# All four column tiles of xr in one pass over the blocks of x, with the norm's sums and row factors inside the last two blocks

## The chip, the cores and the metric

One kernel on one core of a Trainium2 chip. The metric is the device time of one execution in microseconds (us). A kernel is timed in several runs, and its median counts. Beside the times there is one profiled execution, whose trace gives every instruction with start and duration. TensorE is called PE below, its weight loads PEld, VectorE DVE, ScalarE ACT, GpSimd POOL, and SyncE, which here only issues DMAs, SP.

## The reference

One layer of an encoder, for 512 positions and 1024 channels, in float32. What matters here is its beginning:

```
h = rms_norm(x, attn_norm_g)
proj = h @ w_in
xr, gate, q, k, v = jnp.split(proj, [D_RNN, 2 * D_RNN, ...], axis=-1)
xr = centred_depthwise_conv(xr, conv_w, conv_b)
h_f = rg_lru(xr, ..., False)
h_b = rg_lru(xr, ..., True)
y_rnn = (h_f + h_b) * gelu(gate)
```

`x` is 512 x 1024, `w_in` 1024 x 2560; `xr`, `gate`, `q`, `k`, `v` have 512 columns each. Dilated attention over q, k, v, an output projection, an MLP of width 4096 and a final norm follow.

## The kernel before

A float32 product is done as three passes: each operand is split into a part `hi`, rounded to the matmul's format, and the rest `lo`, and the sum `hi*hi + hi*lo + lo*hi` is accumulated (`mm3`, L303 to L305: three matmuls in a row into one PSUM tile). ACT or DVE makes `hi`, DVE makes `lo`.

**The first stage, xr.** x arrives transposed, in eight blocks of 128 channels x 512 positions (`k` = 0 to 7), and each block is followed in the same transfer by 384 columns of `w_in` for it, that is column tiles 0 to 2 of xr (`xw0` for block 0, in two transfers; `xw` for the others, 448 KB each). SP issues these one after the other. `cvx(k)` splits the block: h_hi = x times the norm's gain (ACT; in blocks 0 and 1 ACT and DVE share it), w3h (the weights' hi part), h_lo and w3l on DVE. `sq(k)` squares the block on ACT, `addsq` adds the squares up on DVE. PE goes through the blocks and for each does three mm3, one per column tile `t` (`pxr[0..2]`); in blocks 0 and 1 the passes are ordered by part instead (L435). In the last block, after tile 0, PE transposes the summed squares (`turned`, tile pcs).

**The fourth tile, and the norm's row factor.** Column tile 3 of xr comes from an ordinary weight chunk (`chunks[3]` = w_in[3], 512 KB, `conv_hi(3)`, `conv_lo(3)`; the tiles are wraw for the raw chunk, whi and wlo for its parts). Its eight mm3 (`xmm`) run after the others. DVE sums the transposed squares (`row_sums`, cs), scales (`rstd_cols`, rv), and POOL raises to the power -0.5 (`rcol`, L403). After three of tile 3's blocks PE transposes that column into a row factor (`row_tile`: prow on PE, L395, rrow on ACT, L409).

**What follows.** `conv_a(t)` (L486, DVE, then L488, ACT) multiplies pxr[t] by the row factor and begins the convolution, `conv_b(t)` (L493 to L495, DVE) ends it, tile xc. Meanwhile PE begins the projection of v: 32 steps of one mm3 (tile pv), with chunks 4 to 7. After steps 2, 5, 8 and 11 `lru_gates(t)` (L514, tile pg) does eight small matmuls from xc[t] into four PSUM tiles of the same four banks ("pj") that pxr had. On POOL, the constants of the recurrence (L161 to L173) follow rcol, and after them the loads of `relt` and `oht` (L664, L666), from which the attention's bias table is made (`bias_round` on DVE).

The order of instructions on each engine is the order in which they are written; SP's order is set by a scheduler.

Of the kernel before, what the change touches and what calls it, by code (L numbers as in the profile page):

```python
# [12 lines left out]
FT = mybir.dt.float32  # L13
FR = mybir.dt.float32r
AF = mybir.ActivationFunctionType
OP = mybir.AluOpType

P = 128
S = 512
D = 1024  # L20
KD = D // P
# [80 lines left out]
def hybrid_kernel(ctx: ExitStack, tc, xw0, xw, xn, w_in, w_v, w_out, w_up, w_dn, gates, vecs, rel, onehot, fg, out):  # L102
    nc = tc.nc
    consts = ctx.enter_context(tc.tile_pool(name="consts", bufs=1))
    big = ctx.enter_context(tc.tile_pool(name="big", bufs=1))
    stream = ctx.enter_context(tc.tile_pool(name="stream", bufs=3))
# [9 lines left out]
    def g_(name, dt=FT, shape=(P, S)):  # L116
        return work.tile(list(shape), dt, name=name, tag="g", bufs=NG)
# [4 lines left out]
    def ps_(name, tag):  # L122
        return psum.tile([P, S], FT, name=name, tag=tag, bufs={"pj": 4, "gs": 2, "et": 2}[tag])

    def f(t):
        return t.bitcast(FT)
# [50 lines left out]


    chunks = []
    chunks.extend([None] * 3)  # L180
    chunks.append(w_in[3])
    for kp in range(4):
        chunks.append(w_v[kp])
    for ct in range(4, 8):
# [59 lines left out]
    def conv_hi(i):  # L244
        if i < len(chunks):
            i = swap.get(i, i)
            hi = stream.tile([P, 1024], FR, name="whi", tag="whi", bufs=4)
            if i in ON_DVE:
                nc.vector.tensor_copy(hi, raws[i])
            else:  # L250
                act(hi, raws[i], AF.Copy)  # L251
            splits[i] = (hi,)
# [49 lines left out]
    def mm3(o, a, b, first, last, on=False):  # L302
        nc.tensor.matmul(o, lhsT=a[0], rhs=b[0], start=bool(first), stop=False, skip_group_check=on)  # L303
        nc.tensor.matmul(o, lhsT=a[0], rhs=b[1], start=False, stop=False, skip_group_check=on)  # L304
        nc.tensor.matmul(o, lhsT=a[1], rhs=b[0], start=False, stop=bool(last), skip_group_check=on)  # L305
# [8 lines left out]
    h_hi = big.tile([P, KD, S], FR, name="h_hi", tag="bigA")  # L314
    h_lo = big.tile([P, KD, S], FR, name="h_lo", tag="bigB")

    XW, XG = S + 3 * P, S + KD
    xwt, w3 = [], []
    for k in range(KD):
        if 4 <= k < 7:  # L320
            xwt.append(stream.tile([P, 1024], FT, name="wraw", tag="wraw", bufs=3)[:, :XW])
        else:
            xwt.append(work.tile([P, 1024], FT, name="tw", tag="tw", bufs=4)[:, :XW if k else XG + 3 * P])
        if k == 0:
            nc.sync.dma_start(xwt[0][:, :XG], xw0[:, :XG])
            nc.sync.dma_start(xwt[0][:, XG:], xw0[:, XG:])
        else:
            nc.sync.dma_start(xwt[k], xw[k - 1])
        if k == 6:
            nc.sync.dma_start(vt, vecs)  # L330
# [3 lines left out]
    sqx = {}  # L334

    def cvx(k):
        x, w = xwt[k][:, :S], xwt[k][:, S if k else XG:]
        g = ag[:, k:k + 1] if k else xwt[0][:, S:S + 1]
        hi, lo = g_("w3h", FR), g_("w3l", FR)
        if k < 2:  # L340
            c = (2 * P, 3 * P)[k]
            act(h_hi[:, k, :c], x[:, :c], AF.Copy, scale=g)
            nc.vector.tensor_scalar(h_hi[:, k, c:], x[:, c:], g, None, op0=OP.mult)
            if k == 0:
                nc.vector.tensor_copy(hi[:, :2 * P], w[:, :2 * P])
                act(hi[:, 2 * P:3 * P], w[:, 2 * P:], AF.Copy)
            else:
                nc.vector.tensor_copy(hi[:, :3 * P], w)
        else:
            act(h_hi[:, k, :], x, AF.Copy, scale=g)  # L350
            act(hi[:, :3 * P], w, AF.Copy)
        stt(h_lo[:, k, :], x, g, f(h_hi)[:, k, :], op0=OP.mult, op1=OP.subtract)
        nc.vector.tensor_tensor(lo[:, :3 * P], w, f(hi)[:, :3 * P], op=OP.subtract)
        w3.append((hi, lo))

    def sq(k):
# [22 lines left out]
    def hk(k):  # L379
        return (h_hi[:, k, :], h_lo[:, k, :])  # L380

    def wk(c, k):
        if c < 3:
            return tuple(t[:, c * P:(c + 1) * P] for t in w3[k])
        hi, lo = splits[c]
        return (hi[:, k * P:(k + 1) * P], lo[:, k * P:(k + 1) * P])

    def fan(t, c, n, w):
        base = t[:, c:c + 1]
        return bass.AP(tensor=base.tensor, offset=base.offset, ap=[base.ap[0]] + ([[1, n]] if n > 1 else []) + [[0, w]])  # L390

    def rows_of(cols, tag):
        pr = ps_("prow", tag)
        for tt in range(4):
            nc.tensor.transpose(pr[:, tt * P:(tt + 1) * P], cols(tt), ident)  # L395
        return pr

    def rstd_cols(ssc, n):
        v = small("rv", 4)
        nc.vector.tensor_scalar(v, ssc, 1.0 / n, EPS, op0=OP.mult, op1=OP.add)  # L400
        r = consts.tile([P, 4], FT, name="rcol_%d" % st["rc"])
        st["rc"] += 1
        nc.gpsimd.tensor_tensor(r, v, mhalf, op=OP.pow)  # L403
        return r

    def row_tile(cols, tag):
        pr = rows_of(lambda tt: fan(cols, tt, 1, P), tag)
        r = g_("rrow")
        act(r, pr, AF.Copy)  # L409
        return r  # L410
# [8 lines left out]
    def turned(ss, tag):  # L419
        pc = ps_("pcs", tag)  # L420
        for tt in range(4):
            nc.tensor.transpose(pc[:, tt * P:(tt + 1) * P], ss[:, tt * P:(tt + 1) * P], ident)
        return pc

    def row_sums(pc):
        c = small("cs", 4)
        nc.vector.tensor_reduce(c, pc.rearrange("p (t c) -> p t c", t=4), axis=mybir.AxisListType.X, op=OP.add)
        return c

    pxr = {t: ps_("pxr", "pj") for t in range(3)}  # L430
    for k in range(KD):
        if k < 2:
            for i, (a, b) in enumerate(((0, 0), (0, 1), (1, 0))):
                for t in range(3):
                    nc.tensor.matmul(pxr[t], lhsT=wk(t, k)[a], rhs=hk(k)[b], start=i == 0 and k == 0, stop=False)  # L435
            continue
        for t in range(3):
            mm3(pxr[t], wk(t, k), hk(k), False, k == KD - 1)
            if k == KD - 1 and t == 0:
                sqt = turned(sqx[0], "et")  # L440


    relt = consts.tile([NB3, P], FT, name="relt")
    oht = [work.tile([NB3, S], FT, name="oht", tag="g", bufs=NG) for _ in range(2)]
    nbd = dram.tile([NH, 2 * S], FT, name="nbd")


    ohr = []
# [2 lines left out]
    def bias_round(i):  # L451
        if i == 0:
            r = slice(NBUCK, 2 * NBUCK)
            nc.vector.tensor_copy(relr, relt)
            nc.vector.tensor_tensor(relr[r], relt[r], f(relr)[r], op=OP.subtract)
        t = work.tile([NB3, S], FR, name="ohr", tag="g", bufs=NG)
        ohr.append(t)
        r = slice(3 * NBUCK, NB3)
        nc.vector.tensor_copy(t, oht[i])
        nc.vector.tensor_tensor(t[r], oht[i][r], f(t)[r], op=OP.subtract)  # L460

    def bias_prep():
        for i in range(2):
# [178 lines left out]
            if sub and n >= first and (n - first) % step == 0:  # L642
                sub.popleft()()


    pxr[3] = ps_("pxr", "pj")

    def xmm(ks):
        for k in ks:
            mm3(pxr[3], wk(3, k), hk(k), k == 0, k == KD - 1)  # L650

    for i in (3, 4, 5):
        conv_hi(i)
    conv_lo(3)
    rcol = rstd_cols(row_sums(sqt), D)
    for i in (4, 5):
        conv_lo(i)
    xmm((0, 1, 2))
    rstd = row_tile(rcol, "et")
    conv_a(0, pxr[0])  # L660
    conv_a(1, pxr[1])
    next(spc)
    cneg, chalf = next(spc)
    nc.gpsimd.dma_start(relt, rel)  # L664
    for i in range(2):
        nc.gpsimd.dma_start(oht[i], onehot[:, i * S:(i + 1) * S])  # L666
    xmm((3, 4))
    conv_b(0)
    act(warm, epsb, AF.Sigmoid)
    conv_a(2, pxr[2])  # L670
    xmm((5, 6, 7))
    conv_a(3, pxr[3])
    conv_hi(6)
    conv_b(1)


# [11 lines left out]
        if n in SC:  # L688
            scans.popleft()()

    GATES = {2: 0, 5: 1, 8: 2, 11: 3}
    pv = {}
    vtag = {0: "et", 2: "gs", 3: "gs", 1: "et"}
    steps = [(k, tt) for k in range(KD) for tt in (0, 2, 3, 1)]
    for n, (k, tt) in enumerate(steps):
        c = C_V + k // 2
        if k == 0:
            pv[tt] = ps_("pv", vtag[tt])
        hi, lo = splits[c]
        sl = slice((k % 2) * S, (k % 2 + 1) * S)  # L700
        tsl = slice(tt * P, (tt + 1) * P)
        mm3(pv[tt], (h_hi[:, k, tsl], h_lo[:, k, tsl]), (hi[:, sl], lo[:, sl]), k == 0, k == KD - 1)
        if n >= 16:
            feed(c, n % 8)
        if n in GATES:
            lru_gates(GATES[n])
        if n == 2:
            conv_b(2)
        if n == 6:
            conv_b(3)  # L710
            conv_lo(6)
        if n == 7:
            conv_hi(7)
            conv_lo(7)
        if n in (7, 9):
            bias_round((n - 7) // 2)
        if n == 12:
            conv_hi(8)
            conv_lo(8)
        lru_hooks(n)  # L720
        if n == 20:
            bias_prep()
            load_tw(0)
            load_tw(1)
# [8 lines left out]
    gsteps = [th for t in range(4) for th in proj_thunks(C_G + t, "pj", gate_done(t))]  # L733
    for n, th in enumerate(gsteps):
        th()
        lru_hooks(32 + n)
        if n in (19, 21, 27, 29):
            tt = {19: 0, 21: 2, 27: 3, 29: 1}[n]
            act(vs[:, tt, :], pv[tt], AF.Copy, scale=rcol[:, tt:tt + 1])
# [965 lines left out]
```

## Time and profile before

| | |
|---|---|
| median of 3 runs | 540.11 us (539.92 to 541.29) |
| the profiled execution | 541.17 us |
| its span in the trace | 539.4 us |
| PE busy | 530.2 us of the span |
| DVE, ACT, POOL busy | 433.8, 361.6, 67.5 us |
| transfers | 108 MB, mean 200 GB/s |

The profiled execution lies 1.06 us above the median of the three runs and within their spread; 1.8 us of its time lie outside the span. A busy PE means that a matmul is under way, not that the array is full; matmuls overlap, so the distance from the start of one to the start of the next is what one costs. "<-" after an idle time names what ended it.

### The profile page before, as it was taken

The page shows a single profiled execution, that of the slowest core. Times are in us where ns is not written, and L with a number is a line of the kernel's source. Part 1 is how long each engine was busy: PE and PEld are TensorE (multiplying, and loading weights), DVE is VectorE, ACT ScalarE, POOL GpSimd, SP SyncE. Part 2 cuts the span into 40 slices and gives each one's busy share as a digit, 9 for nine tenths or more (in the row PEclk, how much of TensorE's full clock was granted, in tenths as well). Part 3 has the DMA queues.
Part 4 walks back from the last instruction along what each step waited for, and adds up shares of the span by engine and source line. Part 5 has one row for each costly group of instructions (what it writes and reads, how often), then busy time and mean ns, then how long its engine had stood idle before and what let it go on. Part 6 is the DMA issues. An engine that isn't in the chain of part 4 may idle for free.

```text
span 539.4 us, 8174 instructions
## 1 busy us (share of the span) xinstructions
PE 530.2 (98%) x3007; PEld 450.7 (84%) x3007; DVE 433.8 (80%) x636; ACT 361.6 (67%) x574; POOL 67.5 (13%) x92
## 2 busy tenths in 40 slices
PE   8999999999999999999999999999999999999994
PEld 7856888887886578899999888888999999888884
DVE  5895998996763689889769987879855888987885
ACT  6678965798865746586566755566656777655664
POOL 0173000000001121001030213001101020131000
PEclk9999999999999999999999999999999999999998
DMA  7743386464499698856586799994878397899704
GB/s 274 227 116 123 107 270 190 125 188 159 105 362 254 157 161 229 282 195 175 172 176 176 193 252 275 291 353 111 286 229 204 110 201 194 197 296 261 180 1 156
DMA packets 36664, 108.00 MB, mean 200 GB/s; under 512 B 4484, under 2 KB 7428, under 8 KB 36624
## 3 DMA queue, kind: packets, MB, share of 16 engines
q1 hardware_dynamic: 28480, 78.49, 42.8%
q0 software_dynamic: 7968, 28.76, 28.7%
q8 instruction: 23, 0.38, 0.3%
q10 hardware_dynamic: 176, 0.23, 0.1%
q14 instruction: 17, 0.14, 0.1%
HBM read 98.00 MB, written 4.23 MB: 190 GB/s over the span
## 4 chain that ended last, share of the span: by engine, by line
PE 88%; DMA 4%; DVE 3%; ACT 2%; issue 1%; SPq 0%; DVEq 0%; ACTq 0%
PE pd L303 9%; PE pd L304 9%; PE pd L305 9%; PE pu L305 7%; PE pu L304 7%; PE pu L303 7%; PE pqk L303 3%; DMA tw<-in_w_up_dram 3%; PE pwo L303 3%; PE pqk L305 3%; PE pqk L304 3%; PE pav L897 3%; PE pt L806 3%; PE pwo L305 3%; PE pwo L304 3%; PE pv L303 2%
## 5 line engine op out<-in xcount | busy, mean ns | idle before, releaser
L259 DVE TENSOR_TENSOR wlo<-wraw,whi 128x1024 fp32r<-128x1024 f32 x73 | 89.1, 1221 | 20.6 <-ACT whi L251 20.2
L251 ACT ACTIVATE whi<-wraw 128x1024 fp32r<-128x1024 f32 x70 | 74.0, 1059 | 36.8 <-PE pd L305 19.3
L304 PE MATMUL pd<-wlo,ah 128*128 128x512 f32 (+1 forms) x195 | 75.2, 386 | 0.0
L303 PE MATMUL pd<-whi,ah 128*128 128x512 f32 (+1 forms) x195 | 75.2, 386 | 0.0
L305 PE MATMUL pd<-whi,al 128*128 128x512 f32 (+1 forms) x195 | 75.2, 386 | 0.0
L251 ACT ACTIVATE whi<-tw 128x1024 fp32r<-128x1024 f32 x36 | 38.1, 1060 | 40.8 <-DMA tw<-in_w_up_dram 12.9
L305 PE MATMUL pu<-hh,wlo 128*128 128x256 f32 x224 | 63.4, 283 | 0.0
L304 PE MATMUL pu<-hl,whi 128*128 128x256 f32 x224 | 63.4, 283 | 0.0
L303 PE MATMUL pu<-hh,whi 128*128 128x256 f32 x224 | 63.4, 283 | 0.0
L259 DVE TENSOR_TENSOR wlo<-tw,whi 128x1024 fp32r<-128x1024 f32 x36 | 44.0, 1222 | 20.7 <-ACT whi L251 20.7
L305 PE MATMUL pu<-h2h,wlo 128*128 128x256 f32 (+1 forms) x200 | 60.1, 301 | 0.3 <-DVE wlo L259 0.3
L303 PE MATMUL pu<-h2h,whi 128*128 128x256 f32 (+1 forms) x200 | 60.1, 300 | 0.0
L304 PE MATMUL pu<-h2l,whi 128*128 128x256 f32 (+1 forms) x200 | 60.0, 300 | 0.0
L304 PEld LDWEIGHTS pu<-hl,whi 128*128 128x128 f32 x224 | 43.0, 192 | 0.0
L303 PEld LDWEIGHTS pu<-hh,whi 128*128 128x128 f32 x224 | 43.0, 192 | 0.0
L305 PEld LDWEIGHTS pu<-hh,wlo 128*128 128x128 f32 x224 | 43.0, 192 | 0.0
L305 PEld LDWEIGHTS pd<-whi,al 128*128 128x128 f32 x195 | 36.6, 188 | 7.4
L303 PEld LDWEIGHTS pd<-whi,ah 128*128 128x128 f32 x195 | 36.6, 188 | 7.3
L304 PEld LDWEIGHTS pd<-wlo,ah 128*128 128x128 f32 x195 | 36.6, 188 | 7.3
L251 ACT ACTIVATE whi<-ts 128x1024 fp32r<-128x1024 f32 x24 | 25.5, 1061 | 23.1 <-PE pd L305 18.1
L305 PEld LDWEIGHTS pu<-h2h,wlo 128*128 128x128 f32 x200 | 38.2, 191 | 1.8 <-DVE wlo L259 0.5
L303 PEld LDWEIGHTS pu<-h2h,whi 128*128 128x128 f32 x200 | 38.3, 191 | 1.3
(278 smaller groups left out, 1259.9 us busy)
## 6 DMA issues: line engine op xcount, KB each, us to landing
wraw<-in_w_up_dram SPq DMA_DIRECT2D x25, 512.0 KB, 3.7
ts<-in_w_dn_dram POOLq DMA_DIRECT2D x24, 512.0 KB, 13.1
wraw<-in_w_dn_dram SPq DMA_DIRECT2D x24, 512.0 KB, 9.0
tw<-in_w_up_dram SPq DMA_DIRECT2D x15, 512.0 KB, 10.0
tw<-in_w_up_dram POOLq DMA_DIRECT2D x15, 512.0 KB, 7.4
wraw<-in_w_in_dram SPq DMA_DIRECT2D x13, 512.0 KB, 3.6
ts<-in_w_dn_dram SPq DMA_DIRECT2D x8, 512.0 KB, 4.5
tw<-in_w_dn_dram SPq DMA_DIRECT2D x8, 512.0 KB, 8.9
```

Of the source, the lines that this page charges most:

```text
L251: act(hi, raws[i], AF.Copy)
L259: nc.vector.tensor_tensor(lo, r, f(splits[i][0]), op=OP.subtract)
L303: nc.tensor.matmul(o, lhsT=a[0], rhs=b[0], start=bool(first), stop=False, skip_group_check=on)
L304: nc.tensor.matmul(o, lhsT=a[0], rhs=b[1], start=False, stop=False, skip_group_check=on)
L305: nc.tensor.matmul(o, lhsT=a[1], rhs=b[0], start=False, stop=bool(last), skip_group_check=on)
L806: nc.tensor.transpose(pt[:, qt * P:(qt + 1) * P], en[h][qt][:, jt * P:(jt + 1) * P], ident)
L897: nc.tensor.matmul(pav[p][a, :], lhsT=vs[:, jt, h * DH:(h + 1) * DH], rhs=et.pop((h, jt)), start=jt == 0, stop=jt == 3)
```

## The change

The transfers of x's blocks carry 512 weight columns instead of 384 (512 KB per block; block 0's weights go to a tile of their own, w0t, 256 KB), and chunk 3 falls away. PE does four mm3 per block. The transposes of the squares stand after block 5, those of the row factor after block 6 (in the same PSUM tile, pcs), and the splits of chunks 4, 5 and 6 around them. The loads of relt and oht are written ahead of the loop. In the part on v, an offset `LATER` with value 0 is added to the step numbers, which changes nothing.

```diff
     chunks = []
-    chunks.extend([None] * 3)
-    chunks.append(w_in[3])
+    chunks.extend([None] * 4)
...
+            xwt.append(work.tile([P, 1024], FT, name="tw", tag="tw", bufs=4))
         if k == 0:
             nc.sync.dma_start(xwt[0][:, :XG], xw0[:, :XG])
-            nc.sync.dma_start(xwt[0][:, XG:], xw0[:, XG:])
+            w0t = g_("w0t")
+            nc.sync.dma_start(w0t, xw0[:, XG:])
...
             if k == 0:
                 nc.vector.tensor_copy(hi[:, :2 * P], w[:, :2 * P])
-                act(hi[:, 2 * P:3 * P], w[:, 2 * P:], AF.Copy)
+                act(hi[:, 2 * P:], w[:, 2 * P:], AF.Copy)
             else:
-                nc.vector.tensor_copy(hi[:, :3 * P], w)
+                nc.vector.tensor_copy(hi, w)
         else:
             act(h_hi[:, k, :], x, AF.Copy, scale=g)
-            act(hi[:, :3 * P], w, AF.Copy)
+            act(hi, w, AF.Copy)
         stt(h_lo[:, k, :], x, g, f(h_hi)[:, k, :], op0=OP.mult, op1=OP.subtract)
-        nc.vector.tensor_tensor(lo[:, :3 * P], w, f(hi)[:, :3 * P], op=OP.subtract)
+        nc.vector.tensor_tensor(lo, w, f(hi), op=OP.subtract)
...
+    nc.gpsimd.dma_start(relt, rel)
+    for i in range(2):
+        nc.gpsimd.dma_start(oht[i], onehot[:, i * S:(i + 1) * S])
...
+    pxr = {t: ps_("pxr", "pj") for t in range(4)}
+    for k in range(KD):
+        if k < 2:
+            for i, (a, b) in enumerate(((0, 0), (0, 1), (1, 0))):
+                for t in range(4):
+                    nc.tensor.matmul(pxr[t], lhsT=wk(t, k)[a], rhs=hk(k)[b], start=i == 0 and k == 0, stop=False)
+            continue
+        for t in range(4):
+            mm3(pxr[t], wk(t, k), hk(k), False, k == KD - 1)
+            if (k, t) == (KD - 3, 3):
+                sqt = turned(sqx[0], "et")
+                conv_hi(4)
+                conv_lo(4)
+                rcol = rstd_cols(row_sums(sqt), D)
+                for i in (5, 6):
+                    conv_hi(i)
+                    conv_lo(i)
+            if (k, t) == (KD - 2, 3):
+                rstd = row_tile(rcol, sqt)
...
-    pxr[3] = ps_("pxr", "pj")
-
-    def xmm(ks):
-        for k in ks:
-            mm3(pxr[3], wk(3, k), hk(k), k == 0, k == KD - 1)
-
-    for i in (3, 4, 5):
-        conv_hi(i)
-    conv_lo(3)
-    rcol = rstd_cols(row_sums(sqt), D)
-    for i in (4, 5):
-        conv_lo(i)
-    xmm((0, 1, 2))
-    rstd = row_tile(rcol, "et")
     conv_a(0, pxr[0])
     conv_a(1, pxr[1])
     next(spc)
     cneg, chalf = next(spc)
-    nc.gpsimd.dma_start(relt, rel)
-    for i in range(2):
-        nc.gpsimd.dma_start(oht[i], onehot[:, i * S:(i + 1) * S])
-    xmm((3, 4))
     conv_b(0)
     act(warm, epsb, AF.Sigmoid)
     conv_a(2, pxr[2])
-    xmm((5, 6, 7))
     conv_a(3, pxr[3])
-    conv_hi(6)
     conv_b(1)
```

On POOL, before, from the first column of gains (`ag`) on; rcol is the norm's power, z and the rest the recurrence's constants:

```order
L141 MEMSET mhalf 128x4
L332 COPY ag<-tw 128x8
L403 TENSOR_TENSOR rcol_317<-rv,mhalf 128x4
L161 TENSOR_TENSOR z_173<-z_173,e_171 128x8
...
L173 TENSOR_SCALAR chalf<-sp_172 128x8
L664 DMA relt<-in_rel_dram 97x128
L666 DMA oht<-in_onehot_dram 97x512 x2
```

and in the changed kernel, at the same place:

```order
L141 MEMSET mhalf 128x4
L332 COPY ag<-tw 128x8
L430 DMA relt<-in_rel_dram 97x128
L432 DMA oht<-in_onehot_dram 97x512 x2
L397 TENSOR_TENSOR rcol_317<-rv,mhalf 128x4
L161 TENSOR_TENSOR z_174<-z_174,e_172 128x8
```

The three loads moved from behind the constants to the place right behind `ag`, which waits for block 0's x.

On PE, before, around the transposes of the squares (pcs) and of the row factor (prow); pxr_217 to pxr_219 are tiles 0 to 2, pxr_302 is tile 3:

```order
L305 MATMUL pxr_217<-h_hi_97,w3l_194 128x512
L422 MATMUL pcs_286<-ident_79,sqx_127 128x128 x4
L303 MATMUL pxr_218<-h_hi_97,w3h_193 128x512
...
L305 MATMUL pxr_219<-h_hi_97,w3l_194 128x512
L303 MATMUL pxr_302<-h_hi_97,whi_303 128x512
...
L305 MATMUL pxr_302<-h_hi_97,wlo_309 128x512
L395 MATMUL prow_336<-ident_79,rcol_0_317 128x128 x4
L303 MATMUL pxr_302<-h_hi_97,whi_303 128x512
```

and in the changed kernel (pxr_226 to pxr_229 are tiles 0 to 3; w3h_166, w3h_184 and w3h_194 are the weights of blocks 5, 6 and 7):

```order
L302 MATMUL pxr_229<-h_hi_97,w3h_166 128x512
L303 MATMUL pxr_229<-h_lo_98,w3h_166 128x512
L304 MATMUL pxr_229<-h_hi_97,w3l_167 128x512
L417 MATMUL pcs_302<-ident_79,sqx_128 128x128 x4
L302 MATMUL pxr_226<-h_hi_97,w3h_184 128x512
...
L304 MATMUL pxr_229<-h_hi_97,w3l_185 128x512
L402 MATMUL pcs_302<-ident_79,rcol_0_317 128x128 x4
L302 MATMUL pxr_226<-h_hi_97,w3h_194 128x512
```

Before, 15 matmuls stand between the two groups of transposes and another 15 between the second group and the first of v; now 12 and 12. Both groups moved ahead of the end of the stage, the first from block 7 to block 5.

## Rows read from the trace of the kernel before

**Rows 1.** The page's first lines: busy us of each engine.

```profile
PE 530.2 (98%) x3007; PEld 450.7 (84%) x3007; DVE 433.8 (80%) x636; ACT 361.6 (67%) x574; POOL 67.5 (13%) x92
```

**Rows 2.** Waits of PE, whole span: us in total, times, longest.

```profile
PE pwarm L146 <- DVE epsb L137: 1.0, 1, 1.0
PE pxr L435 <- ACT h_hi L342: 0.8, 1, 0.8
PE pu L305 <- DVE wlo L259: 0.3, 1, 0.3
```

**Rows 3.** The chain that ended last, its beginning: start us, us, what.

```profile
1.64 6.07 DMA tw<-in_xw_dram
7.80 0.62 ACT h_hi L342
8.51 2.38 PE pxr L435 x9
```

**Rows 4.** Timeline of PE: start us, us, instruction, [idle before].

```profile
4.48 1.63 PE L435 MATMUL pxr<-h_hi,w3h 128*128 128x512 f32 x3
...
8.51 0.94 PE L435 MATMUL pxr<-h_hi,w3h 128*128 128x512 f32 x3 [0.77 <-ACT h_hi L342]
...
10.73 0.39 PE L303 MATMUL pxr<-h_hi,w3h 128*128 128x512 f32 x1
...
21.61 0.60 PE L422 MATMUL pcs<-ident,sqx 128*128 128x128 f32 x4
...
25.48 0.60 PE L395 MATMUL prow<-ident,rcol 128*128 128x128 f32 x4
...
29.35 0.39 PE L303 MATMUL pv<-whi,h_hi 128*128 128x512 f32 x1
...
31.48 1.95 PE L514 MATMUL pg<-xc,gwr 64*64 64x512 f32 x16
```

**Rows 5.** DMA queues between 2 and 7.7 us: packets, MB, share of the engines.

```profile
q1 hardware_dynamic: 644, 1.65, 90.5%
```

**Rows 6.** DMA queues between 45 and 47.6 us, POOL's queue.

```profile
q0 software_dynamic: 191, 0.45, 54.5%
```

**Rows 7.** Timeline of POOL.

```profile
3.53 0.19 POOL L332 COPY ag<-tw 128x8 f32<-128x8 f32 x1 [2.18 <-DMA tw<-in_xw_dram]
23.30 1.88 POOL L403 TENSOR_TENSOR rcol<-rv,mhalf 128x4 f32<-128x4 f32 x1 [19.59 <-DVE rv L400]
...
43.51 0.84 POOL L664 DMA_DIRECT2D relt<-in_rel_dram  x1
```

**Rows 8.** Timeline of DVE.

```profile
3.98 0.29 DVE L345 CAST w3h<-tw 128x256 fp32r<-128x256 f32 x1
...
7.81 0.29 DVE L343 TENSOR_SCALAR h_hi<-tw,ag 128x128 fp32r<-128x128 f32 x1 [2.41 <-DMA tw<-in_xw_dram]
8.01 0.35 DVE L348 CAST w3h<-tw 128x384 fp32r<-128x384 f32 x1
...
9.12 0.55 DVE L353 TENSOR_TENSOR w3l<-tw,w3h 128x384 fp32r<-128x384 f32 x1
...
10.78 0.68 DVE L361 TENSOR_TENSOR sqx<-sqx 128x512 f32<-128x512 f32 x1
...
21.00 1.22 DVE L259 TENSOR_TENSOR wlo<-wraw,whi 128x1024 fp32r<-128x1024 f32 x1
...
26.75 1.29 DVE L486 TENSOR_TENSOR xr<-pxr,rrow 128x512 f32<-128x512 f32 x2 [1.01 <-ACT rrow L409]
27.95 0.16 DVE L159 TENSOR_SCALAR z<-e 128x8 f32<-128x8 f32 x1
...
30.56 1.28 DVE L486 TENSOR_TENSOR xr<-pxr,rrow 128x512 f32<-128x512 f32 x2
```

**Rows 9.** The instructions of line 403, ns min/median/max.

```profile
L403 POOL TENSOR_TENSOR rcol<-rv,mhalf x3: 1048/1144/1878, 23.3 to 192.7; 128x4 f32<-128x4 f32 x3
```

**Rows 10.** Waits of DVE up to 75 us.

```profile
DVE relr L454 <- DMA relt<-in_rel_dram: 5.4, 1, 5.4
```

More of the change, by code (lines that the diff above doesn't have):

```diff
@@ L315, in hybrid_kernel @@
     h_lo = big.tile([P, KD, S], FR, name="h_lo", tag="bigB")
-    XW, XG = S + 3 * P, S + KD
+    XG = S + KD
     xwt, w3 = [], []
@@ L320, in hybrid_kernel @@
         if 4 <= k < 7:
-            xwt.append(stream.tile([P, 1024], FT, name="wraw", tag="wraw", bufs=3)[:, :XW])
+            xwt.append(stream.tile([P, 1024], FT, name="wraw", tag="wraw", bufs=3))
         else:
-            xwt.append(work.tile([P, 1024], FT, name="tw", tag="tw", bufs=4)[:, :XW if k else XG + 3 * P])
+            xwt.append(work.tile([P, 1024], FT, name="tw", tag="tw", bufs=4))
         if k == 0:
             nc.sync.dma_start(xwt[0][:, :XG], xw0[:, :XG])
-            nc.sync.dma_start(xwt[0][:, XG:], xw0[:, XG:])
+            w0t = g_("w0t")
+            nc.sync.dma_start(w0t, xw0[:, XG:])
         else:
@@ L336, in cvx @@
     def cvx(k):
-        x, w = xwt[k][:, :S], xwt[k][:, S if k else XG:]
+        x, w = xwt[k][:, :S], xwt[k][:, S:] if k else w0t
         g = ag[:, k:k + 1] if k else xwt[0][:, S:S + 1]
@@ L382, in wk @@
     def wk(c, k):
-        if c < 3:
+        if c < 4:
             return tuple(t[:, c * P:(c + 1) * P] for t in w3[k])
@@ L390, in fan @@
         return bass.AP(tensor=base.tensor, offset=base.offset, ap=[base.ap[0]] + ([[1, n]] if n > 1 else []) + [[0, w]])
[L392 to L396, printed above, removed]
     def rstd_cols(ssc, n):
@@ L404, in rstd_cols, with row_tile @@
         return r
-    def row_tile(cols, tag):
-        pr = rows_of(lambda tt: fan(cols, tt, 1, P), tag)
+    def row_tile(cols, pr):
+        for tt in range(4):
+            nc.tensor.transpose(pr[:, tt * P:(tt + 1) * P], fan(cols, tt, 1, P), ident)
         r = g_("rrow")
@@ L428, in row_sums @@
         return c
[L430 to L440, printed above, removed]
     relt = consts.tile([NB3, P], FT, name="relt")
@@ L689, in lru_hooks @@
             scans.popleft()()
-    GATES = {2: 0, 5: 1, 8: 2, 11: 3}
+    LATER = 0
+    GATES = {LATER + 2: 0, LATER + 5: 1, LATER + 8: 2, LATER + 11: 3}
     pv = {}
@@ L706, in hybrid_kernel @@
             lru_gates(GATES[n])
-        if n == 2:
+        if n == LATER + 2:
             conv_b(2)
-        if n == 6:
+        if n == LATER + 6:
             conv_b(3)
-            conv_lo(6)
-        if n == 7:
+        if n == LATER + 7:
             conv_hi(7)
             conv_lo(7)
-        if n in (7, 9):
-            bias_round((n - 7) // 2)
-        if n == 12:
+        if n in (LATER + 7, LATER + 9):
+            bias_round((n - LATER - 7) // 2)
+        if n == LATER + 12:
             conv_hi(8)
             conv_lo(8)
-        lru_hooks(n)
-        if n == 20:
+        lru_hooks(n - LATER)
+        if n == LATER + 20:
             bias_prep()
@@ L735, in hybrid_kernel @@
         th()
-        lru_hooks(32 + n)
+        lru_hooks(32 + n - LATER)
         if n in (19, 21, 27, 29):
@@ L1662 @@
     xT = a["x"][0].T.reshape(KD, P, S)
-    wx = wi[:, :3 * P].reshape(KD, P, 3 * P)
+    wx = wi[:, :S].reshape(KD, P, S)
     arrs["xw0"] = cont(np.concatenate([xT[0], cols(a["attn_norm_g"][0]), wx[0]], axis=1))
```

## The prediction

> **What bounds the kernel now.** I read the page's first lines, then TensorE's waits, then the beginning of the chain that ended last, and last the timelines of PE, DVE and POOL up to 50 us, where everything that the change touches lies. PE is under way for 530.2 of 539.4 us [rows 1], and over the whole span it waits for another engine three times: 1.0 us before its first matmul, 0.8 us before block 1 of xr, 0.3 us much later [rows 2]. So the kernel is PE's queue of matmuls, and a change that leaves their number as it is can give back only those waits, and can add new ones. The number stays: 8 blocks x 4 tiles x 3 passes = 96 matmuls of 512 columns for xr, the same transposes, the same rest. Only the pauses are to be added up. The reader is to see in the chain that block 1 sets the start: its transfer is issued at 1.64 us and lands 6.07 us later, at 7.71; ACT rounds it from 7.80, PE goes on at 8.51 [rows 3], having stood still for 0.77 us [rows 4]. From there to the first matmul of v at 29.35 PE has no gap. In steady flow a matmul costs (21.61 - 10.73) / 48 = 0.227 us (48: five blocks of nine, and the first three of block 7) [rows 4].
>
> **The pause before block 1.** Four terms.
>
> First, block 0 now has 12 matmuls instead of 9. The three extra ones are done in the pause and are missing later: -3 x 0.227 = -0.68. That holds as long as the pause is longer than they are; block 0 ended at 8.51 - 0.77 = 7.74, and as the first matmuls are slow (three in 1.63, some 0.5 each, against 0.227 [rows 4]) I expect its new end at 8.6 to 8.9.
>
> Second, block 1's first pass needs its weights rounded by DVE: the cast of 256 columns takes 0.29, of 384 columns 0.35 [rows 8], so 512 take about 0.41: +0.06.
>
> Third, more bytes ahead. Block 0's weights and block 1 grow by 64 KB each, 0.13 MB. Between 2 and 7.7 us the DMA engines move 1.65 MB, 0.29 MB a us, at 90.5% of their time [rows 5]. If transfers were served strictly in turn: 0.13 / 0.29 = 0.45. But 1.65 MB are more than blocks 0 and 1 have (0.92), so later blocks move alongside; if all of what moves grows by a seventh, 0.24 / 0.29 = 0.82. At the rate of POOL's stretch below (0.45 MB in 1.42 us, 0.32 a us) it would be 0.41. Bounds 0.4 and 0.8; I take 0.5, near the served-in-turn end.
>
> Fourth, POOL's three loads. They now stand behind the copy of the gains, which ends at 3.53 + 0.19 = 3.72 [rows 7], in the middle of the blocks' transfers. Before, they ran from 45 us on, with hardly anything beside them, and took 54.5% of 2.6 us of all engines, 1.42 us [rows 6]; the first was issued at 43.51 [rows 7], so data flow some 1.5 to 2 us after the issue. In the new place that is 5.2 to 5.7, and block 1, late by the terms above, lands at 8.3 or after. The engines are 90.5% full there [rows 5], so 0.2 or 0.3 us of the 1.42 find room. The bounds are 0 (if the blocks that are already queued go first) and 1.42 (if all of it is served first). I take 1.0, nearer to the upper, since the software queue shares the same engines and has its own packets ready two to three us before block 1 is through. The Trainium skill, in DMA: Bandwidth & Descriptors, section Queues, rings and completion order, says that a DMA engine with work from several queues takes a packet from each in turn. By that rule nearly all of the 1.42 goes ahead of block 1, and the sum below would be 0.4 higher. No stretch of this trace has both queues full, so it does not show it.
>
> Together: -0.68 + 0.06 + 0.5 + 1.0 = +0.9; PE starts block 1 near 9.4 + 0.7 = 10.1 us.
>
> **Row factor: a new wait.** Time is counted from DVE's first instruction on block 1 (7.81 before, [rows 8]). DVE works without a gap from there to chunk 3's subtraction at 21.00, 13.19 later. Each of blocks 1 to 7 now subtracts 512 columns of weights instead of 384: 0.68 instead of 0.55 [rows 8], 7 x 0.13 = 0.93, and the cast 0.06: +0.99. The subtraction there is now chunk 4's, of the same size, and still stands ahead of the row sums. From its start to the end of POOL's power it took 23.30 + 1.88 - 21.00 = 4.18 [rows 7, 8]. So rcol is ready at 13.19 + 0.99 + 4.18 = 18.36. PE gets to the second transposes at 0.70 + 0.06 (start) + 2.90 (block 1: 10.73 - 8.51 = 2.22 for nine, three more at 0.227) + 60 x 0.227 = 13.6 (blocks 2 to 6) + 0.47 (the first transposes: 25.48 - 21.61 = 3.87 less fifteen matmuls) = 17.73. It waits 0.63, and 0.1 for the hand-over (ACT's end at 8.42 to PE's start at 8.51 [rows 3]): +0.7. Before, PE came to this point just late enough; there the power had ended at 25.18 and PE was there at 25.48. What is queued behind: block 7's 12 matmuls and all of v. Bounds: the power took 1.05 to 1.88 in its three uses [rows 9]; with 1.05 the wait is 0, and with a DVE that is 0.2 later it is 0.9. The first transposes wait for nothing by the same count: squares ready at 14.2, PE there at 17.73 - 0.47 - 2.72 = 14.5.
>
> **The gates.** The row factor reaches DVE 26.75 - 25.48 = 1.27 after the transposes start; now 18.46 + 1.27 = 19.7, when tile 0's last matmul ends too (18.46 + 0.47 + 0.68 + 0.16). From there the two first conv_a and conv_b(0) take 30.56 - 26.75 = 3.81 [rows 8], 0.1 more because tile 1 ends 0.68 later: 23.6. xr ends on PE at 18.46 + 0.47 + 2.72 = 21.65, and the gates come 31.48 - 29.35 = 2.13 after [rows 4], at 23.8. That is a near miss, where before there was 0.9 of room. The last conv_a ends 1.28 later still, at 24.9, and the fourth PSUM tile of the gates is wanted near 25.1. I put 0.1, bounds 0 and 0.5.
>
> **At nothing.** Chunk 3 goes: 512 KB, one rounding on ACT, one subtraction of 1.22 on DVE, against 7 x 0.13 added there; the sums on both engines stay, and PE does not wait for them afterwards [rows 2]. ACT's roundings grow as well, by 128 columns a block as DVE's subtractions do; before, DVE went into the first chunk's subtraction at 21.00 without waiting for ACT [rows 8], and DVE falls back by no less than ACT. Chunks 4 to 6 are asked for one place earlier in SP's queue. DVE's wait of 5.4 us for relt [rows 10] goes; it hid behind the matmuls of v, and PE did not wait for the bias table, so nothing is gained; were that cover gone, up to 5.4 would be.
>
> **Sum.** +0.9 + 0.7 + 0.1 = +1.7 on the profiled execution's 541.17. That one was 1.06 above the median; the pauses are the same in both, so I add the sum to 540.11: 541.8. All lower bounds give -0.62 + 0.4 = -0.2, all upper ones -0.62 + 0.8 + 1.42 + 0.9 + 0.5 = +3.0.
>
> **Rivals.** (a) POOL's loads do not delay block 1, the queued blocks go first. Then the fourth term is 0: +0.7, 540.8, within 0.3% (1.6 us, about what a measurement can tell here) and not slower. It decides below 0.9 us of delay: there the sum falls under 1.6. For it: data of POOL's queue come late. Against: 90% full engines. (b) The power is quick or the row sums come early and PE does not wait at the row factor: +1.0, 541.1, no change that can be told. (c) The change gains: only if neither new wait exists and the bytes ahead cost less than 0.4; -0.6 at best, 539.5, still within 0.3%; to be faster by more there is no pause left to give back. (d) The longer pause before block 1, about 1.5 us instead of 0.77, brings PE's clock back to its lower level of 1.2 GHz. The first three matmuls of block 0 went at some 0.5 each against 0.227 later, and after the 0.77 us they went on at the fast spacing within block 1 (9 in 2.22) [rows 4]; twelve slow ones would cost 12 x 0.27 = 3.3: 545.1.
>
> **Chances.** My forecast, both waits, 0.52, its own range 541.0 to 543.0; (a) 0.2; (b) 0.15; (c) 0.07; (d) 0.06. A bit over 0.6 of the first lies above the 0.3% bound of 541.7, and (d); (a), (b), (c) nearly all within. So slower 0.42, same 0.54, faster 0.04. For 8 in 10 I take 540.4 to 543.1.
>
> **What would show it.** PE's wait before block 1 in the new trace: about 1.3 to 1.6 us, with POOL's queue moving its 0.45 MB between 5 and 9 us. A wait of PE at the row factor's transposes for rcol of about 0.7. The gates waiting for DVE 0 to 0.3. No other wait of PE up to 60 us, and the same distances from there to the end. I am wrong if block 1 lands before 8.5, if PE waits for the squares, or if the time after the gates differs.

## The result and the profile after

The changed kernel takes 541.01 us (median of 14 runs, 540.14 to 541.58); the kernel before, beside it, 540.01 us (14 runs, 539.41 to 541.29). The ratio is 1.0016, 95% interval 1.0009 to 1.0023: 1.0 us or 0.2% slower. Forecast were 541.8 us, within 540.4 to 543.1. The size came out near, but not by the steps that the prediction gave: the pause before block 1 got shorter instead of longer, a wait that the prediction had counted out took its place, and the kernel's last microseconds got shorter too.

The waits of PE over the whole span of the changed kernel (us in total, times, longest), beside [rows 2]:

```profile
PE pwarm L146 <- DVE epsb L137: 1.0, 1, 1.0
PE pcs L417 <- DVE sqx L361: 0.9, 1, 0.9
PE pcs L402 <- POOL rcol L397: 0.5, 1, 0.5
PE pxr L454 <- DVE w3h L348: 0.3, 1, 0.3
```

Of the 0.77 us before block 1, 0.28 are left. Two waits are new: PE stands at the transposes of the squares (L417) until DVE has added them up, and at those of the row factor (L402) until POOL has raised them to the power. PE's timeline of the same kernel shows what each costs, beside [rows 4]:

```profile
4.48 1.74 PE L454 MATMUL pxr<-h_hi,w3h 128*128 128x512 f32 x4
...
8.33 1.17 PE L454 MATMUL pxr<-h_hi,w3h 128*128 128x512 f32 x4 [0.28 <-DVE w3h L348]
...
21.82 0.39 PE L304 MATMUL pxr<-h_hi,w3l 128*128 128x512 f32 x1
23.12 0.63 PE L417 MATMUL pcs<-ident,sqx 128*128 128x128 f32 x4 [0.91 <-DVE sqx L361]
...
26.11 0.39 PE L304 MATMUL pxr<-h_hi,w3l 128*128 128x512 f32 x1
27.01 0.65 PE L402 MATMUL pcs<-ident,rcol 128*128 128x128 f32 x4 [0.52 <-POOL rcol L397]
...
30.27 0.39 PE L302 MATMUL pv<-whi,h_hi 128*128 128x512 f32 x1
...
32.47 2.23 PE L521 MATMUL pg<-xc,gwr 64*64 64x512 f32 x16
34.62 0.50 PE L302 MATMUL pv<-whi,h_hi 128*128 128x512 f32 x1
```

The distance from start to start is what counts. A matmul takes 0.227; from 21.82 to the first transposes are 1.30, so 1.07 are lost; from 26.11 to the second 0.90, so 0.67 are lost. The first gates take 34.62 - 32.47 = 2.15, where before it was 1.88, and come 2.20 instead of 2.13 after v's start: 0.34 lost. Now the sum: block 1 starts 0.18 earlier than before (8.33 against 8.51), which is less than this start differs between two traces of one kernel (below); from there to v it is 21.94 instead of 20.84, that is 1.10 more (1.07 + 0.67, less 0.68 for three matmuls that block 0 did ahead, and 0.04 of small differences); 0.34 at the gates. -0.18 + 1.10 + 0.34 = 1.26 at the end of the first gates, and the same 1.3 at the first matmul of the last projection (pd, 299.9 against 298.6). Up to there nothing is given back.

At the very end something is. The last output transfer is issued here before, where the span ends at 539.4, and here in the changed kernel, where it ends at 539.2:

```profile
535.12 0.38 SPq L1387 DMA_DIRECT2D out_dram<-ot  x1
```

```profile
535.76 0.38 SPq L1373 DMA_DIRECT2D out_dram<-ot  x1
```

From the end of that issue to the end of the span it is 3.90 us before and 3.06 now. This is no scatter: the five traces of kernels with the order of before have 3.88 to 3.91, the seven with the changed order 3.00 to 3.08 (all runs below included). Why the end is 0.85 shorter stays open; no run was made for it. The two profiled executions, 541.17 and 540.98, differ by another 0.6 inside pd, which takes 233.4 from its first matmul to its last before and 232.8 now. The granted clock of the last 20 us was 0.90 and 0.98, but five other traces with 0.92 there have 232.7 or 232.8 as well, so that the clock made the 0.6 is not shown.

Why the squares come late is seen on ACT and DVE, in the changed kernel's timelines:

```profile
7.55 0.62 ACT L342 ACTIVATE h_hi<-tw,ag 128x384 fp32r<-128x384 f32 x1 [2.58 <-DMA tw<-in_xw_dram]
...
11.51 0.72 ACT L350 ACTIVATE h_hi<-tw,ag 128x512 fp32r<-128x512 f32 x1 [0.92 <-DMA tw<-in_xw_dram]
...
13.72 0.72 ACT L350 ACTIVATE h_hi<-wraw,ag 128x512 fp32r<-128x512 f32 x1 [0.44 <-DMA wraw<-in_xw_dram]
```

```profile
12.27 0.75 DVE L352 SCALAR_TENSOR_TENSOR h_lo<-tw,ag,h_hi 128x512 fp32r<-128x512 f32 x1 [0.73 <-ACT h_hi L350]
...
14.48 0.75 DVE L352 SCALAR_TENSOR_TENSOR h_lo<-wraw,ag,h_hi 128x512 fp32r<-128x512 f32 x1 [0.25 <-ACT h_hi L350]
...
22.89 1.22 DVE L258 TENSOR_TENSOR wlo<-wraw,whi 128x1024 fp32r<-128x1024 f32 x1
```

Blocks 3 and 4 were not there when ACT wanted them. DVE lost 0.73 + 0.25 = 0.98 behind ACT and carried that to the squares; before, it had no gap between 7.81 and 21.00 [rows 8]. What came in between is seen in POOL's timeline, and in the DMA queues (packets, MB, share of the engines), between 2 and 8, between 9 and 10, and between 8 and 12 us, beside [rows 6, 7]:

```profile
3.60 0.86 POOL L430 DMA_DIRECT2D relt<-in_rel_dram  x1
4.46 1.15 POOL L432 DMA_DIRECT2D oht<-in_onehot_dram  x2
```

```profile
q1 hardware_dynamic: 661, 1.95, 93.9%
q0 software_dynamic: 7, 0.02, 0.7%
```

```profile
q1 hardware_dynamic: 46, 0.18, 63.1%
q0 software_dynamic: 46, 0.11, 39.6%
```

```profile
q1 hardware_dynamic: 236, 0.86, 68.5%
q0 software_dynamic: 176, 0.42, 36.2%
```

POOL's loads (q0) were issued from 3.60 on, but of their packets only 7 moved before 8 us; nearly all moved between 8 and 12, from 9 to 11 about one for one with the blocks' packets (q1). That is behind block 1 and in front of blocks 3 and 4.

### The profile page after: what moved, and what is told of

It reads as the page before. It is cut to its first block, busy times and chain, and to the rows that moved or that the text cites. A ratio compares the mean times of both kernels' runs of the same rounds, so it can differ in the third digit from the quotient of the medians.

```text
span 539.2 us, 8169 instructions
## 1 busy us (share of the span) xinstructions
PE 530.3 (98%) x3007; PEld 450.6 (84%) x3007; DVE 434.3 (81%) x635; ACT 362.4 (67%) x573; POOL 67.3 (12%) x92
## 4 chain that ended last, share of the span: by engine, by line
PE 94%; DVE 2%; DMA 2%; issue 0%; SPq 0%; POOL 0%; ACT 0%; DVEq 0%; ACTq 0%; POOLq 0%
PE pu L304 10%; PE pu L302 10%; PE pu L303 10%; PE pd L303 9%; PE pd L304 9%; PE pd L302 9%; PE pqk L302 3%; PE pwo L302 3%; PE pqk L304 3%; PE pqk L303 3%; PE pav L883 3%; PE pt L792 3%; PE pwo L304 3%; PE pwo L303 3%; DMA wraw<-in_xw_dram 2%; PE pv L302 2%
## 5 line engine op out<-in xcount | busy, mean ns | idle before, releaser
L258 DVE TENSOR_TENSOR wlo<-wraw,whi 128x1024 fp32r<-128x1024 f32 x72 | 87.9, 1220 | 23.7 <-ACT whi L250 23.4
L302 PE MATMUL pu<-h2h,whi 128*128 128x256 f32 (+1 forms) x200 | 60.1, 300 | 0.0
L303 PEld LDWEIGHTS pu<-h2l,whi 128*128 128x128 f32 x200 | 38.3, 191 | 1.3
```

Source lines behind the costliest of these rows:

```text
L258: nc.vector.tensor_tensor(lo, r, f(splits[i][0]), op=OP.subtract)
```

## The experiments

Three theories were put to the test for the wait at the squares: A, POOL's early loads hold up blocks 3 and 4; B, the wider blocks do; C, DVE's own added work does. Two questions came with them: what the factor and the gates hang on, and whether block 1's landing was moved by the change at all. "Before" in each comparison is the kernel before on the same chip, 540.26 to 540.51 us.

**POOL's loads back in their old place**, run twice:

```diff
-    nc.gpsimd.dma_start(relt, rel)
-    for i in range(2):
-        nc.gpsimd.dma_start(oht[i], onehot[:, i * S:(i + 1) * S])
...
     cneg, chalf = next(spc)
+    nc.gpsimd.dma_start(relt, rel)
+    for i in range(2):
+        nc.gpsimd.dma_start(oht[i], onehot[:, i * S:(i + 1) * S])
```

> The changed kernel with POOL's loads of relt and oht back behind the recurrence's constants, all else as changed. Theory A (the early loads share the DMA engines with blocks 3 and 4, hold up ACT and DVE by 1.0 us, and so PE at the transposes of the squares): ACT waits for no block after block 1, PE's loss at the squares falls from 1.07 us to 0.2 or less, the loss at the row factor stays 0.6 to 0.8, and the kernel takes 1.0 us less than the changed one, 540.0. Rival B (blocks 3 and 4 come late because each block has 512 KB instead of 448): ACT's waits of 0.92 and 0.44 stay, the loss at the squares stays near 1.0, 541.0. Rival C (DVE's own added work of 0.99 us makes the squares late): ACT's waits go, but at least 0.6 of the loss at the squares stays, 540.5 or more.

> The changed kernel with POOL's loads back in their old place, a second time, beside the changed kernel on the same chip. By theory A it is 1.0 us below the changed kernel (0.2%) and within 0.3 of the kernel before; if block 1 lands later without the early loads (7.66 and 7.96 in two traces of such kernels, 7.46 and 6.34 with them), part of that is given back, 0.4 to 0.7. Rival B or C: no difference between the two.

Measured: 540.15 us, ratio to the kernel before 1.0004 (0.9986 to 1.0022), and the second time 539.92, 0.9997 (0.9985 to 1.0009). PE's waits in the first trace:

```profile
PE pwarm L146 <- DVE epsb L137: 1.0, 1, 1.0
PE pxr L451 <- DVE w3h L348: 0.6, 1, 0.6
PE pcs L402 <- POOL rcol L397: 0.4, 1, 0.4
PE pu L304 <- DVE wlo L258: 0.2, 1, 0.2
```

The wait at the squares is gone in both traces, ACT waits for no block after block 1, and of the two new waits only the factor's is left. From block 1 to v it is 20.70 and 20.71 us instead of 21.94. Theory A; B and C fall, since the blocks are as wide and DVE's work as much as in the changed kernel. What the loads took from the blocks is seen in the first trace's queues between 8 and 12 us, beside those of the changed kernel above:

```profile
q1 hardware_dynamic: 492, 1.63, 102.0%
```

The engines are full in both, but with both queues at work they moved 0.86 + 0.42 = 1.28 MB in these 4 us, without POOL's loads 1.63. So the loads cost the blocks' queue 0.77 MB, nearly twice their own 0.42. The other traces agree: 1.23 to 1.33 MB with the early loads (four traces), 1.63 to 1.68 in the eight without.

**The changed kernel again**, on the same chip as the second of these:

> The changed kernel itself, on the same chip as the run with the late loads beside it. If block 1's landing (7.46 in its first trace) is scatter of the chip, it may lie anywhere from 6.3 to 8.0, with the same losses behind it: about 1.0 at the squares, 0.6 to 0.7 at the factor, 0.3 at the gates, and POOL's data between 7.5 and 12.5 us. If the early loads bring block 1 forward, it lands below 7.5 again. Time: 1.0 above the kernel before.

Measured: 541.08, ratio 1.0004 (0.9995 to 1.0014). Its ratio alone does not tell it from the kernel before; its median is 1.16 above that of the late loads beside it (11 runs each, with ranges that overlap: 539.67 to 541.63 and 539.29 to 541.48). The means of these runs differ by 0.76, by their scatter something between 0.2 and 1.4. Its trace repeats the first: 0.94 and 0.50 of waiting, 21.94 from block 1 to v, 4.36 from v to the end of the first gates.

**The early loads alone, in the kernel before**, run twice:

```diff
     nbd = dram.tile([NH, 2 * S], FT, name="nbd")
+    nc.gpsimd.dma_start(relt, rel)
+    for i in range(2):
+        nc.gpsimd.dma_start(oht[i], onehot[:, i * S:(i + 1) * S])
...
-    nc.gpsimd.dma_start(relt, rel)
-    for i in range(2):
-        nc.gpsimd.dma_start(oht[i], onehot[:, i * S:(i + 1) * S])
```

> The kernel before with one edit, POOL's three loads issued right behind the copy of the gains. Theory A: blocks 3 and 4 land about 1 us later than before, DVE falls back by about 1 us, PE waits some 0.4 at the squares and 0.2 at the row factor and perhaps 0.2 within block 3; 0.7 us slower than before. Rival B: the loads find room, no wait of ACT for a block after block 1, time as before within 0.2 us. By the prediction's own fourth term, block 1 itself would land 1.0 us later than the 7.71 of before; by the trace of the changed kernel, where POOL's data flow only from 7.9 us on, it lands at 7.4 to 7.8.

> The kernel before with the early loads, a second time. In its first trace block 1 landed at 6.3 instead of 7.7 and PE then lost 0.64 us between block 1 and v against the kernel before. If that landing is scatter, it comes now between 7 and 8 and the kernel is 0.4 to 0.7 us above the one before; if the early loads bring it forward, it lands near 6.4 again, and the time is as before within 0.3.

Measured: 540.31, ratio 0.9999 (0.9989 to 1.0010), and 540.20, 0.9999 (0.9988 to 1.0010). PE's waits in the first trace:

```profile
PE pwarm L146 <- DVE epsb L137: 1.0, 1, 1.0
PE pcs L422 <- DVE sqx L361: 0.4, 1, 0.4
```

The mechanism is there: ACT waits 1.7 and 1.1 us for blocks after block 1, PE waits 0.4 and 0.2 at the squares, and from block 1 to v it takes 21.48 and 21.52 us, 0.6 to 0.7 more than before (20.84). The row factor's wait, expected with 0.2, is not there. The time does not show the loss. In both traces PE started block 1 early, at 7.58 and 7.46; that makes up for it against the first trace of the kernel before (8.51), but not against its second (7.62, below). So the expected 0.7 us was missed in the time and met from block 1 to v.

**The wider transfers alone, in the kernel before:**

```diff
-            xwt.append(work.tile([P, 1024], FT, name="tw", tag="tw", bufs=4)[:, :XW if k else XG + 3 * P])
+            xwt.append(work.tile([P, 1024], FT, name="tw", tag="tw", bufs=4))
...
-            nc.sync.dma_start(xwt[0][:, XG:], xw0[:, XG:])
+            w0t = g_("w0t")
+            nc.sync.dma_start(w0t, xw0[:, XG:])
...
-        x, w = xwt[k][:, :S], xwt[k][:, S if k else XG:]
+        x, w = xwt[k][:, :S], xwt[k][:, S:S + 3 * P] if k else w0t[:, :3 * P]
...
-    wx = wi[:, :3 * P].reshape(KD, P, 3 * P)
+    wx = wi[:, :S].reshape(KD, P, S)
```

> The kernel before with the wider transfers alone: each block's rows carry 512 weight columns (4 KB a row; block 0's weights in a tile of their own), the computation still reads 384 of them and loads chunk 3 as before. By the prediction's third term block 1 lands 0.5 us later, at 8.2, and the kernel is 0.5 us slower. By the trace of the changed kernel, where block 1 landed at 7.46 with more bytes ahead of it, rows of 4 KB cost nothing here: 7.4 to 7.8, time as before within 0.3 us. Rival B of the run with the late loads (wider blocks make blocks 3 and 4 late) would show ACT waiting 0.5 or more for blocks 3 and 4 here.

Measured: 540.80, ratio 1.0010 (0.9998 to 1.0022). Block 1 landed at 7.87, ACT waited for no later block, and PE's only wait inside the stage is this one:

```profile
PE pxr L436 <- ACT h_hi L343: 1.8, 1, 1.8
```

Theory B falls here too. Whether the wider rows cost half a microsecond at block 1 this run does not settle: its interval reaches from nothing to 1.2 us.

**Row sums ahead of chunk 4's subtraction**, added to the late loads:

```diff
                 conv_hi(4)
-                conv_lo(4)
                 rcol = rstd_cols(row_sums(sqt), D)
+                conv_lo(4)
```

> As the run with late loads, and DVE's row sums and scaling stand ahead of the subtraction of chunk 4 instead of behind it. If the row factor is late because that subtraction (1.22 us) stands ahead of the sums, the factor is ready 0.6 us earlier (the sums then wait for PE's transposes for some 0.5), and PE's loss there falls from about 0.7 to 0.2 or less: 539.5, which is 0.5 below the kernel before. Rival: POOL's power sets it, or the subtraction is wanted elsewhere (v's first step): the loss stays or reappears ahead of v, 540.0.

Measured: 539.87, ratio 0.9991 (0.9981 to 1.0001). PE still waits 0.25 at the factor; from block 1 to v it is 20.56, 0.14 less than with the late loads alone. The subtraction was not what held the sums up for long: DVE now waits 0.9 us for PE's transposes ahead of the sums. The 0.5 us expected were not there.

**The factor's transposes three matmuls later, and v's steps one later:**

```diff
-            if (k, t) == (KD - 2, 3):
+            if (k, t) == (KD - 1, 0):
                 rstd = row_tile(rcol, sqt)
...
-    LATER = 0
+    LATER = 1
```

> As the run with the sums first, with the row factor's transposes three matmuls later (after tile 0 of block 7 instead of after block 6) and everything that is hung on v's steps one step later (the offset LATER is 1 instead of 0). If the waits left there are a matter of place alone, PE's wait for the factor (0.25) and its late weight load (some 0.2) go, the first gates take 1.9 us instead of 2.15, and no wait comes up elsewhere: 0.7 less than the run with the sums first, about 0.2% below the kernel before. Rival: DVE's convolutions come later with the factor and the gates wait for them just as long: 0.3 less at most.

Measured: 539.96, ratio 0.9990 (0.9980 to 1.0001). PE waits nowhere in the stage; from block 1 to v it is 19.97, and the first gates end 4.92 after v's start, one step of 0.68 included. So 0.7 us were won up to there, as expected. But from the first pp to the first pt it takes 52.9 us (58.9 to 111.8) instead of 52.2 with the sums first (60.4 to 112.6): 0.7 is lost again. In that stretch PE's weight loads wait for DVE (the tiles qs and mn of the attention), and in the run with the sums first they wait for nothing there:

```profile
PEld ps L768 <- DVE qs L755: 1.0, 3, 0.4
PEld ps L768 <- DVE mn L781: 0.3, 1, 0.3
```

**The same without the later steps:**

```diff
-    LATER = 1
+    LATER = 0
```

> As the run with the factor and the gates later, but with the steps hung on v back in their place (LATER is 0). That run took 0.6 us less from block 1 to v than the run with the sums first and then lost 0.8 between the first ps (95.6 us) and the first pt (111.8 us), with PE's weight loads waiting for DVE. If the shifted steps cause that loss (they put DVE's work on the recurrence one step later), it goes here: the first pt comes 51.5 us after the first pp, as in the other traces, the 0.6 us stay, 539.5 or less. If DVE is the bound there and the loss comes from PE's earlier arrival, it stays near 0.8 whatever the steps, and the time is 539.9 to 540.2. The gates wait for DVE at most 0.5 longer than in the run with the sums first.

Measured: 539.99, ratio 0.9994 (0.9985 to 1.0003). PE's waits:

```profile
PE pwarm L146 <- DVE epsb L137: 1.0, 1, 1.0
PE pg L518 <- ACT warm L657: 0.6, 1, 0.6
```

The name behind the second is that of the semaphore that came last by the profile, an ACT instruction that ended at 30.94; PE goes on at 31.18, after DVE's third step of conv_b(0), which begins at 30.32 and lasts 0.75, to 31.07. From the first pp to the first pt it takes 52.1 us again (60.1 to 112.2; the 51.5 of the expectation was a miscount, the other traces have 52.2), so the loss is gone. But this does not tell the shifted steps from PE's earlier arrival as its cause, because PE did not come early here: its first pp stands 51.8 us after the start of block 1, as with the sums first (51.6), against 50.8 with the later steps. The factor's wait has only moved: 20.12 to v, and 4.92 from there to the end of the gates, without an extra step.

**The kernel before once more, for its trace:**

> The kernel before once more, for its trace alone. Block 1 landed at 7.71 in its first trace, and in the nine others, of kernels with and without the early loads and the wider blocks, between 6.3 and 8.0. If that is scatter of the chip, it may lie anywhere between 6.3 and 8.0 here; from the start of block 1 on PE to v it takes 20.8 us again.

One run, 539.86. PE starts block 1 at 7.62, 0.89 earlier than in the first trace of the same kernel; from there to v it takes 20.90, and 4.00 to the end of the first gates. The traces together (us; PE's start of block 1, from there to the first matmul of v, from there to v's first matmul behind the gates):

```
kernel                        block 1   to v    through the gates
before                          8.51    20.84   4.01
before, again                   7.62    20.90   4.00
wider transfers alone           8.68    20.90   4.01
early loads alone               7.58    21.48   4.01
early loads alone, again        7.46    21.52   4.01
changed                         8.33    21.94   4.35
changed, again                  8.54    21.94   4.36
changed, loads late             8.53    20.70   4.35
changed, loads late, again      7.89    20.71   4.36
  and sums first                8.83    20.56   4.36
  and factor later              8.29    20.12   4.92
  and v's steps one later       8.06    19.97   4.92 (one step of 0.68 in it)
```

The first column differs by up to 0.9 us between two traces of one kernel (8.51 and 7.62); the other two repeat within 0.06. In its second trace the kernel before has no pause before block 1 at all:

```profile
PE pwarm L146 <- DVE epsb L137: 1.0, 1, 1.0
```

So the 0.77 us in which block 0 was to hide three more matmuls are themselves part of that scatter. By its time none of the kernels made for these runs is told apart from the kernel before; all their intervals hold 1.

## Why the prediction came out as it did

**What bounds the kernel: right.** Up to the end the change in time is the change in PE's pauses, and the shift at the end of the first gates, 1.26 us, is still there at 299.9 us. "The same distances from there to the end" failed in the last 4 us, which are 0.85 shorter; the sum had nothing there.

**The pause before block 1, +0.9: wrong, and in its fourth term.** The three extra matmuls were hidden in this trace: block 0 ends at 8.05 (8.6 to 8.9 were expected), and the pause fell from 0.77 to 0.28. But where block 1 comes early, as in the second trace of the kernel before, there is no pause to hide them in. PE was to start block 1 near 10.1 and started it at 8.33. POOL's loads, put at 1.0 us with bounds of 0 and 1.42, delayed block 1 by nothing that the traces show: in the wide kernels ACT begins block 1 at 7.55 and 7.76 with the early loads, and between 6.81 and 8.05 in the six traces with late ones. The failed step is the time from issue to data, 1.5 to 2 us. It was read behind the issue at 43.51, where the other queue took 68% of the engines until 45, and carried over to a place where they were full. There, counted from the first issue, it was over 4 us for nearly all packets, and block 1 had landed.

The trace of before could have told this. It has a load that POOL issued while the other queue was full; the queues are those between 158 and 160, between 160 and 161, and between 161 and 162 us:

```profile
158.08 0.99 POOL L986 DMA_DIRECT2D ws<-in_w_out_dram  x1 [18.44 <-PE ps L783]
```

```profile
q1 hardware_dynamic: 230, 0.83, 103.5%
```

```profile
q1 hardware_dynamic: 197, 0.38, 99.0%
q0 software_dynamic: 1, 0.00, 2.0%
```

```profile
q1 hardware_dynamic: 329, 0.20, 63.7%
q0 software_dynamic: 28, 0.11, 57.3%
```

One packet moved within 2.9 us of the issue, the rest later. What makes POOL's packets late when the other queue is full, no run here isolates. The prediction's remark that no stretch of that trace has both queues full is wrong as well. Between 330 and 340 us they are:

```profile
q0 software_dynamic: 380, 1.38, 69.3%
q1 hardware_dynamic: 380, 1.36, 36.2%
```

The Trainium skill's rule that was weighed there (DMA: Bandwidth & Descriptors, section Queues, rings and completion order: each engine takes a packet from each queue in turn) agrees with this, 380 packets to 380, and with 46 to 46 between 9 and 10 us in the changed kernel. It holds for packets that are there to be taken, and before 8 us POOL's hardly were.

**The third term, +0.5 for the bytes: open.** ACT begins block 1 at 6.39 to 7.80 in the four traces with 384 columns (mean 6.95) and at 6.81 to 8.05 in the eight with 512 (mean 7.56). The means differ by 0.6, each group scatters by more, and the one run made for it has an interval from -0.02% to +0.22%.

**The squares, "wait for nothing": wrong.** The count had DVE ready at 14.2 and PE there at 14.5 after DVE's start, a margin of 0.3, and took for granted that DVE would go through without a gap, as before. DVE lost 0.98 to blocks 3 and 4, and PE 1.07. So a price of the loads was there, and close to the 1.0 that stood in the sum, but at another place and through another chain: blocks 3 and 4, ACT, DVE's backlog, the squares. That the total came near is luck in good part: by the trace the sum was 1.7 too high at block 1 and 0.85 too high at the end, and 1.07 too low at the squares. The single traces scatter too much at block 1 to add up to the measured 1.0. All three signs that the prediction named for being wrong came: block 1 landed before 8.5, PE waited for the squares, and the time after the gates differs.

**The row factor, +0.7: right,** 0.67 in the trace, although DVE came there 0.98 later than counted: PE had just been held up at the squares for about as long. With the late loads 0.54 is lost there. The bound was rightly named as DVE's and POOL's chain; that chunk 4's subtraction in it matters less than its 1.22 us, because the sums then wait for the transposes, the run with the sums first showed.

**The gates, +0.1: too small,** 0.34, within the bounds of 0 and 0.5. The chain from the factor over conv_a and conv_b(0) was right, and so was the near miss. That this place is tight is shown by the run with the factor later, in which the 0.44 saved up to v against the sums first came back here as 0.56.

**The rivals.** (a), block 1 undelayed, is what happened, but without its consequence. Without the early loads the new order yields nothing and costs nothing that the time can tell (540.15 and 539.92): the 0.68 us that block 0 hides are spent at the factor (0.54) and the gates (0.34), where the new order leaves less room, and the shorter end does not show in the time. The slowdown is that of the early loads in the wider stage: moving them back takes 1.2 us from the stage in both traces. Alone, in the kernel before, they cost 0.6 to 0.7 us in the traces from block 1 to v and nothing that the time shows; whether block 1's early start in both of these traces has to do with them stays open (ACT begins it at 6.39 and 6.69 there, and at 7.80 and 6.91 in the kernel as it was).

**The chances.** Slower was given 0.42; by the prediction's own parts, a bit over 0.6 of 0.52 and the 0.06 of (d), it is below 0.4. Nothing else hangs on it.

## What to carry to other kernels

When a transfer is moved ahead, ask not only what it delays first but which later transfer it meets, and follow the engine that consumes that one: a backlog of a microsecond shows up where another engine waits for its sum, not where the data came late. A margin of a few tenths on a chain that has been gapless so far is no margin if its feed changes. And a wait that hangs on a chain of another engine is not removed by asking for its result later: it moves to the next thing that hangs on the same chain.

## What the runs showed of the hardware

Block 1's transfer lands with a scatter of its own: issued at 1.64 or 1.65 us in each trace, it was taken up by ACT at 7.80 and 6.91 in two traces of one unchanged kernel, and between 6.39 and 8.05 over twelve.

Loads that POOL issued at 43.5, while the other queue took 68% of the engines, moved data from 45 us on. Issued at 3.6 behind the blocks that SP had queued, with over 90% taken, nearly all of them moved after 8 us, until 12 or 13; in the other three traces with the early loads at most 4 packets moved before 8. At 158.1, with the engines full, one packet moved within 2.9 us.

Where both queues had packets, they moved about one for one (380 to 380 between 330 and 340 us of the kernel before). The engines then moved less in all: 1.23 to 1.33 MB between 8 and 12 us, against 1.63 to 1.68 from one queue alone.
